# Layer A's keys and queries 2 to 5 as seven-part block products

## The chip, the cores and the metric

The kernel runs on one core of a Trainium2 chip. The core has five engines with a queue each: TensorE (PE; its weight loads are shown apart as PEld), VectorE (DVE), ScalarE (ACT), GpSimd (POOL) and SyncE (SP), which here only issues DMAs. Each queue is worked off in order, and an instruction at the head of a queue that waits holds up all that are behind it. The metric is the device time of one execution in microseconds (us).

## The reference

A decoder trunk of two layers over 1024 tokens of width 1024 in float32. The part that matters here is the first layer's projection of the normed stream `h`, which gives 16 query heads of 64, and keys and values for three branches of attention (compressed blocks, selected blocks, a window) with four groups each:

```python
proj = h @ w_in
splits = [D_MODEL + i * KV_DIM for i in range(7)]
q, kc, vc, ks, vs, kwn, vwn, gl = jnp.split(proj, splits, axis=-1)
...
k_cmp = compress(kvh(kc), pe_k, w1_k, w2_k)
v_cmp = compress(kvh(vc), pe_v, w1_v, w2_v)
```

`compress` cuts the tokens into overlapping blocks of 32, adds `pe`, and sends each through a matrix `w1` of 2048 x 256, a Gelu and a small `w2`. The attention over the three branches, the output projections, the feed-forward parts and the second layer follow; they are the same in both kernels.

## The kernel before

**Numbers in two parts.** A float32 operand is held as a main part (H, a rounded copy made by ACT) and a rest (L, the difference, made by VectorE); `split` makes them. A product is three matmuls: main by main, rest by main, main by rest (`mm3`). The turned stream lies as hT: eight tiles hH0 to hH7 (128 of the 1024 features by 1024 tokens) and eight rests hL0 to hL7.

**Projections.** `proj_T` (line 270) makes 128 columns of `h @ w_in`, turned: for each half of the tokens (512) 8 x 3 matmuls of 128x512 into a bank "mm" (there are six). One chunk of 128 columns holds two heads. Its weights come through `Weights.load` (line 191): one DMA into `wraw`, then wh by ACT and wl by VectorE, in rings of 3, 5 and 5 tiles. The result is split again and stored to DRAM by `store_heads` (line 405) as two tiles, sth and stl, of two buffers each: kS for keys, qS for queries.

**The stage.** hT is made in two halves; the compressed keys' input (kc2) and the values vS of the window follow; then the compression of the keys (`compress`, line 527, with i = 0), the values of the selected blocks, the compressed values' input, and the compression of the values (i = 1). A compression has 16 steps: ACT makes bh (128x256), VectorE bl, both in two buffers, and PE runs six matmuls of 128x256 into two banks, "cmp0" and "cmp1". The second compression is cut into parts by a generator (`steps`), and after each part comes a projection: query chunk 0, key chunk 0 of the selected blocks, key chunk 0 of the window, query chunk 1. Then the pools of the compression close, and key chunks 1 and query chunks 2 to 5 follow with nothing between. Query chunks 6 and 7 come later, between the first steps of the attention.

**Work beside it.** `out_blocks` (line 457) prepares the two output matrices for products that come much later: eight times two tiles ob of 128x1024 are loaded, combined by four subtractions on VectorE, and stored to wS. There are two buffers for each of the two tiles. `next(made)` moves this on by one block, and the loop's order in the text says where. The attention's first loads (queries Q, keys KW and K, bias T) go to tiles of the pools aA0, aA1 and aP, which lie where the tiles of this stage were, so a load waits for the last reader of what lay there.

**What sets the order.** The program is written in the order above; a scheduler then puts each engine's instructions in an order of its own when the kernel is built, and on the chip that order is fixed. `after(x)` asks it to put an instruction no earlier than x.

The seven-part block product is used in later stages already: `cols_steps` (line 1147) makes, from four blocks of a weight matrix (512 features by 128 columns) and prepared sums of the turned rows, four blocks of a result with seven products of 12 matmuls, m1 to m7, in place of eight.

Of the kernel before, what the change touches and what calls it, by code (L numbers as in the profile page):

```python
# [14 lines left out]
OP = mybir.AluOpType  # L15
# [114 lines left out]
def trunk(ctx, tc, I, out):  # L130
# [43 lines left out]
    on_pool, on_vector = [None], [None]  # L174

    def split(H_, L_, src, scale=None, eng=None):

        if scale is None:
            prev = nc.scalar.activation(H_, src, AF.Copy)
            rest = (eng or nc.vector).tensor_sub(L_, src, f32(H_))  # L180
            (on_vector if eng is None else on_pool)[0] = rest
        else:
            prev = nc.scalar.activation(H_, src, AF.Copy, scale=scale)
            nc.vector.scalar_tensor_tensor(L_, src, scale, f32(H_), op0=OP.mult, op1=OP.subtract)
# [85 lines left out]
    def proj_T(w, hT, evac, parts=((0, 512), (512, S))):  # L270

        (wh, wl), (hH, hL) = w, hT
        for lo, hi in parts:
            ps = bank("mm")[:, :hi - lo]
            tk = slice(lo, hi)
            for k in range(KC):
                mm3(ps, (wh[:, k], wl[:, k]), (hH[k][:, tk], hL[k][:, tk]), k == 0, k == KC - 1)
# [150 lines left out]
    with ExitStack() as c:  # L428
# [3 lines left out]
        sv = pool(vctx, "pvt", "right")  # L432
        cctx = ExitStack()
# [23 lines left out]
        def out_blocks(places):  # L457
# [3 lines left out]
            for n in range(9):  # L461
                if ready is not None:
                    dst, ((b11, b12), (b21, b22)), b = ready
# [5 lines left out]
                    for r in range(2):  # L469
                        nc.gpsimd.dma_start(dst[r], b[r])  # L470
                if n == 4:
                    yield
                if n < 8:
                    w, i = (I["a_w_out"][0], I["b_w_out"][0])[n // 4], n % 4
                    b = [places[0].tile([128, 1024], F32, name=f"ob{r}", bufs=2) for r in range(2)]
                    for r in range(2):
                        with after(wts.last):
                            nc.sync.dma_start(b[r], w[(i + 4 * r) * 128:(i + 4 * r + 1) * 128, :])
                    ready = wS[n // 4][i], [(t[:, :512], t[:, 512:]) for t in b], b
                yield  # L480

        def evac_v(i):
            def f(t, ps):
                vt = sv.tile([128, G, DH], F32, name="vt", bufs=2)
# [89 lines left out]

        tok_proj(wv, 304, hT, natural, evac_v(1), range(4, NT))
        places_ = [pool(cctx, "po")]
        made = out_blocks(places_)
# [6 lines left out]
        nc.scalar.activation(gates, gates, AF.Sigmoid)  # L584
        tok_proj(wide(wts, W[:, 1792:2048], 256, 4), 256, hT, natural, evac_v(0))
        next(made)
        for _ in steps:
            pass
        kc2 = blocks_tile()
# [3 lines left out]
        next(made)  # L593

        def evac_k(i, ch):
            def f(ps, tk):
                t = [st.tile([128, 512], F32R, name=n, bufs=2) for n in ("sth", "stl")]
                split(*t, ps)
                store_heads(lambda b, z: kS[i, 2 * ch + b, z], t, tk)
            return f  # L600

        def store_blockind():
            for a in range(2):
                cols = slice(a * 512, (a + 1) * 512)
                raw = sv.tile([16, 512], F32, name="bif", bufs=1)
                nc.gpsimd.dma_start(raw, I["blockind"][:, cols])
                t = st.tile([128, 512], F32R, name="sth", bufs=2)
                nc.scalar.copy(t[:16], raw)
                nc.gpsimd.dma_start(bS[:, cols], f32(t[:16]))

        def evac_q(ch):
            def f(ps, tk):
                t = [st.tile([128, 512], F32R, name=n, bufs=2) for n in ("sth", "stl")]
                split(*t, ps, -DH ** -0.5)
                store_heads(lambda b, z: qS[2 * ch + b, z * 64:(z + 1) * 64], t, tk)
            return f

        def proj_k(i, ch):
            c0 = (1536, 2048)[i] + 128 * ch
# [1345 lines left out]
```

## Time and profile before

| what | value |
|---|---|
| time, median of 3 runs | 2793.09 us (2792.3 to 2796.37) |
| the profiled execution | 2793.83 us, its span 2792.1 us |
| mean granted TensorE clock | 0.997 |
| PE busy | 2738.9 us, 98% of the span |
| VectorE, ACT, POOL busy | 79%, 51%, 50% |
| chain that ended last | PE 85%, VectorE 6%, ACT 2%, issue 2%, DMA 2% |
| DMA | 315.13 MB, mean 113 GB/s |

Busy shares are means over stages. [...] A line such as `bh<-kc,pet 128x256 ... x22 | 16.1, 749 | 10.6 <-PE` is a group of 22 instructions that write bh from kc and pet: 16.1 us in all, 749 ns each, with 10.6 us of idle time of that engine ahead of them that PE ended. In a timeline, a row has start, duration, engine, line, operation, tiles, shapes and count, and in square brackets the engine's idle time before it. "To landing" is the time from the issue of a DMA until its data are there.

### The profile page before, as it was taken

The numbers are of one execution on the slowest core, as the hardware profiler recorded it, in microseconds if no ns is written. First come the engines' busy times: TensorE is split into PE (matmuls) and PEld (weight loads), VectorE is DVE, ScalarE is ACT, GpSimd is POOL, SyncE is SP. The second block draws the span as 40 slices with busy tenths as digits, with TensorE's granted clock in tenths as the row PEclk, the third lists the DMA queues.
The fourth block names the chain that finished last, engine by engine and source line by source line (L and its number), as shares of the span: only waits on it lengthen the run. The fifth ranks groups of instructions, "written<-read, shape, count | busy, mean of one in ns | idle before, by whom it ended". The sixth has DMA issues, their size and how long they took to land.

```text
span 2792.1 us, 43025 instructions
## 1 busy us (share of the span) xinstructions
PE 2738.9 (98%) x14494; PEld 2218.9 (79%) x14494; DVE 2214.7 (79%) x4527; ACT 1426.8 (51%) x3171; POOL 1402.8 (50%) x1454
## 2 busy tenths in 40 slices
PE   9999999999999999999999999999999999999997
PEld 8988676776788888888778888777778888888886
DVE  5453888887889899989875677688898888888987
ACT  5531777775644343333454444577756433343434
POOL 3135655552465566565457787110014756655652
PEclk9999999999999999999999999999999999999999
DMA  8669443224122322232224555786341211112112
GB/s 237 218 196 298 133 128 105 68 62 159 35 76 69 83 65 68 62 77 62 84 80 116 167 156 159 242 257 187 114 174 44 74 58 57 49 57 61 54 42 83
DMA packets 292924, 315.13 MB, mean 113 GB/s; under 512 B 50428, under 2 KB 229677, under 8 KB 292704
## 3 DMA queue, kind: packets, MB, share of 16 engines
q1 hardware_dynamic: 272240, 249.40, 30.5%
q0 software_dynamic: 20464, 62.99, 7.4%
q8 instruction: 115, 1.88, 0.3%
q14 instruction: 105, 0.86, 0.1%
HBM read 243.96 MB, written 81.95 MB: 117 GB/s over the span
## 4 chain that ended last, share of the span: by engine, by line
PE 85%; DVE 6%; ACT 2%; issue 2%; DMA 2%; POOL 1%; SPq 1%; POOLq 0%; DVEq 0%; ACTq 0%
PE ux L1161 18%; PE uy L1161 15%; PE dx L993 8%; PE o L390 7%; PE pt L353 6%; PE dr L993 6%; PE dr L1161 4%; PE mm L230 3%; PE mm L229 3%; PE mm L231 3%; PE s L758 1%; DVE pl L954 1%; PE s L846 1%; PE s L1808 1%; PE s L845 1%
## 5 line engine op out<-in xcount | busy, mean ns | idle before, releaser
L954 DVE TENSOR_TENSOR pl<-oT,ph 128x512 fp32r<-128x512 f32 x340 | 340.2, 1018 | 72.3 <-PE dr L993 17.4
L953 ACT ACTIVATE ph<-oT 128x512 fp32r<-128x512 f32 x346 | 211.8, 628 | 215.6 <-PE ux L1161 53.3
L954 DVE TENSOR_TENSOR pl<-oTb,ph 128x512 fp32r<-128x512 f32 x232 | 214.7, 948 | 27.2 <-PE dr L993 17.4
L953 ACT ACTIVATE ph<-oTb 128x512 fp32r<-128x512 f32 x238 | 145.5, 628 | 168.7 <-PE ux L1161 53.4
L353 PE MATMUL pt<-ident,P 128*128 128x128 f32 x1536 | 228.0, 278 | 3.3 <-DVE pT L356 1.9
L742 POOL TENSOR_SCALAR P<-P,sm,gates 128x384 f32<-128x384 f32 (+7 forms) x256 | 183.2, 727 | 79.3 <-DVE sm L740 54.8
L353 PEld LDWEIGHTS pt<-ident,P 128*128 128x128 f32 x1536 | 172.9, 140 | 61.8 <-issue 43.0
L998 DVE TENSOR_TENSOR xrfx<-xrfx,dr 128x512 f32<-128x512 f32 x320 | 204.2, 679 | 17.8 <-PE dr L993 17.7
L1354 POOL TENSOR_TENSOR oT<-oT,gffn 128x512 f32<-128x512 f32 x92 | 118.9, 1303 | 196.0 <-DMA oT<-in_ffn_w_up_dram 127.7
L998 DVE TENSOR_TENSOR xrfx<-xrfx,dx 128x512 f32<-128x512 f32 x320 | 204.5, 678 | 2.2 <-PE dx L993 2.2
L738 ACT ACTIVATE P<-P,m 128x384 f32<-128x384 f32 (+7 forms) x256 | 171.1, 670 | 36.0 <-DVE m L851 14.9
L356 DVE COPY pT<-pt 128x512 f32<-128x512 f32 (+1 forms) x224 | 143.2, 648 | 44.5 <-PE pt L353 39.8
L1354 POOL TENSOR_TENSOR oTb<-oTb,gffn 128x512 f32<-128x512 f32 x92 | 111.8, 1226 | 130.8 <-DMA oTb<-in_ffn_w_up_dram 79.0
L356 ACT COPY pT<-pt 128x512 f32<-128x512 f32 x192 | 110.1, 578 | 103.8 <-PE pt L353 100.8
L390 PE MATMUL o<-pT,V 128*64 128x256 f32 x1200 | 160.7, 391 | 2.3 <-ACT pT L356 1.5
L1770 ACT ACTIVATE P<-P,st 128x384 f32<-128x384 f32 (+2 forms) x256 | 139.6, 548 | 32.3 <-DVE st L1765 30.4
L1765 DVE CUSTOM_DVE_ANT_0 P<-s,T 128x384 f32<-128x384 f32 (+2 forms) x256 | 112.9, 478 | 10.5 <-PE pt L353 3.0
L390 PEld LDWEIGHTS o<-pT,V 128*64 128x64 f32 x1200 | 73.6, 136 | 51.8 <-issue 9.9
L993 PE MATMUL dx<-ph 128*128 128x512 f32 x320 | 107.5, 390 | 0.8 <-ACT ph L953 0.8
L993 PE MATMUL dx<-ph,pl 128*128 128x512 f32 x320 | 107.0, 389 | 0.0
L847 DVE CUSTOM_DVE_ANT_0 P<-s,T 128x128 f32<-128x128 f32 (+3 forms) x192 | 99.5, 550 | 8.1 <-PE s L846 7.8
L230 PE MATMUL mm<-hL,wh 128*128 128x512 f32 (+1 forms) x272 | 102.6, 378 | 0.0
(623 smaller groups left out, 8040.3 us busy)
## 6 DMA issues: line engine op xcount, KB each, us to landing
qB<-xrfx POOLq DMA_DIRECT2D x96, 256.0 KB, 4.5
oT<-in_ffn_w_up_dram SPq DMA_DIRECT2D x92, 256.0 KB, 2.9
oTb<-in_ffn_w_up_dram SPq DMA_DIRECT2D x92, 256.0 KB, 2.9
Q<-qB SPq DMA_DIRECT2D x40, 512.0 KB, 6.9
wd<-in_ffn_w_down_dram SPq DMA_DIRECT2D x60, 256.0 KB, 2.6
oT<-in_b_w_q_dram SPq DMA_DIRECT2D x48, 256.0 KB, 5.6
K<-kBs SPq DMA_DIRECT2D x40, 256.0 KB, 7.5
wraw<-in_a_w_in_dram SPq DMA_DIRECT2D x18, 512.0 KB, 6.9
```

Of the source, the lines that this page charges most:

```text
L230: nc.tensor.matmul(ps, lh, rl, start=False, stop=False, skip_group_check=bool(shared))
L353: prev = nc.tensor.transpose(ps[:, i * 128:(i + 1) * 128], h, ident)
L356: copy(t[:, :w], ps[:, :w])
L390: mm = nc.tensor.matmul(po[64 * e:64 * e + 64, :256], v[e], t, start=first and lo == i == 0, stop=last and hi == nb and i == len(ops) - 1, ...
L738: nc.scalar.activation(P[:, e, :n], P[:, e, :n], AF.Exp, bias=mm[:, e:e + 1], scale=-1.0, accum_out=sm[:, e:e + 1])
L742: nc.gpsimd.tensor_scalar(P[:, e, :n], P[:, e, :n], sm[:, e:e + 1], gate(e), op0=OP.mult, op1=OP.mult)
L953: nc.scalar.activation(h, src, AF.Copy)
L954: self.last = (eng or nc.vector).tensor_sub(l, src, f32(h))
L993: nc.tensor.matmul(banks[t], part(a, t)[u], b[v], start=z == 0 and onX != 2, stop=z == 2, skip_group_check=True)
L998: nc.vector.tensor_add(xs, xs, banks[t])
L1161: mm = nc.tensor.matmul(b, x[:, i * 128:(i + 1) * 128], ys[i], start=first and (z, i) == (0, 0), stop=(z, i) == (2, 3), skip_group_check=True)
L1354: nc.gpsimd.tensor_mul(v, v, gains[:, k:k + 4].unsqueeze(2).to_broadcast([128, 4, 128]))
```

## The change

Four jobs take the place of eight of the projections, each two chunks wide (256 columns): the selected blocks' keys (0 and 1), the window's keys (0 and 1), queries 2 and 3, queries 4 and 5. A job is one `cols_steps`: its blocks of weights W11, W12, W21, W22 (two chunks by two halves of the features) and their sums are multiplied with halves of hT. B11, B12, B21 and B22 are the halves of the features by halves of the tokens, and need no work; T1 = B12 - B11, T2 = B22 - T1, T3 = B22 - B12 and T4 = B21 - T2 are made once, in two parts each, by `block_sums`. Query chunks 0 and 1 stay as they were, 0 ahead of the second compression and 1 in two halves among the jobs.

```diff
-    def proj_T(w, hT, evac, parts=((0, 512), (512, S))):
+    def proj_T(w, hT, evac, parts=((0, 512), (512, S)), prev=None, where="mm"):
...
     def store_heads(dst, t, cols):
         for b in range(2):
-            for z in range(2):
-                nc.gpsimd.dma_start(dst(b, z)[:, cols], f32(t[z][b * 64:(b + 1) * 64]))
+            nc.gpsimd.dma_start(dst(b)[:, :, cols], f32(t[b * 64:(b + 1) * 64]))
+
+    def two_parts():
+        t = st.tile([128, 2, 512], F32R, name="st", bufs=2)
+        return t, (t[:, 0, :], t[:, 1, :])
...
+        def full():
+            return [f32(t) for t in two_parts()[1]]
+
+        def difference(x, y):
+            t, u = full()
+            with after(on_rest[0]):
+                nc.vector.tensor_sub(t, f32(x[0][:]), f32(y[0][:]))
+            with after(on_rest[0]):
+                nc.vector.tensor_sub(u, f32(x[1][:]), f32(y[1][:]))
+            nc.vector.tensor_add(t, t, u)
+            return t
...
+                if names == "T1":
+                    t = difference(o("B12"), o("B11"))
+                    split(*o("T1"), t)
+                    u, _ = full()
+                    nc.vector.tensor_sub(u, f32(o("B22")[0]), t)
+                    nc.vector.tensor_add(u, u, f32(o("B22")[1]))
+                    split(*o("T2"), u)
+                else:
+                    split(*o(names), difference(*map(o, dict(T3=("B22", "B12"), T4=("B21", "T2"))[names])))
...
+        place = [lambda r: full()]
+        made = out_blocks(place)
...
+        block_sums("T1")
+        block_sums("T3", range(3))
...
         steps = compress(1, kc2, wts)
-        for n, (f, a) in enumerate(((proj_q, (0,)), (proj_k, (0, 0)), (proj_k, (1, 0)), (proj_q, (1,)))):
-            f(*a)
-            if n % 2 == 1:
-                next(made)
-            next(steps, None)
+        proj_q(0)
         for _ in steps:
             pass
+        q1 = wts.load(W[:, 128:256], KC, 128)
...
+        R_, H_, L_ = [[r.tile() for _ in range(n)] for r, n in zip(wts.rings, (3, 4, 4))]
+        cutin = lambda *ts: [t[:, k:k + 512] for t in ts for k in (0, 512)]
+        pairs = Given(list(zip(cutin(*H_[:2]), cutin(*L_[:2]))))
+        wu = Turns(cutin(*R_) + [f32(t) for t in cutin(H_[3])])
...
+        load_job(0)
+        load_job(1)
+        block_sums("T3", (3,))
+        block_sums("T4")
+        fs = [job(n) for n in range(len(jobs))]
...
+                ob = [f32(r.tile()[:]) for r in wts.rings[1:]]
+                place[0] = lambda r: ob[r]
...
+        seq = fs[0][:4] + fs[1][:4] + [lambda: plain(0)] + fs[0][4:6] + [with_load(fs[0][6], 2, False), lambda: plain(1)]
+        seq += fs[1][4:5]
+        end = fs[1][5:]
+        for n in range(2, len(jobs)):
+            seq += [with_load(fs[n][0], len(jobs)), fs[n][1]] + end[:-1] + [with_load(end[-1], n + 1)] + fs[n][2:4] + [with_load(fs[n][4], len(jobs))]
+            end = fs[n][5:]
+        staged(seq + end)
...
-            proj_k(0, 1)
-            proj_k(1, 1)
-            next(made)
-            proj_q(2)
-            next(made)
-            proj_q(3)
-            proj_q(4)
-            next(made)
-            proj_q(5)
-            next(made)
...
-        rKs = Ring("K", [128, S], F32R, [(kA0, 2)])
+        rKs = Ring("K", [128, S], F32R, [(kA1, 2)])
```

`cols_steps`, `Pairs` and `staged` move up in the file; `cols_steps` takes the engine of its sums as an argument, and here it is VectorE. A step m is split in two: `prep` makes the pair of its weights (`wh` by ACT, `wl` by VectorE, in four pairs of half tiles that take turns), `run` its 12 matmuls; `staged` writes the preparation of a step ahead of the matmuls of the one before. The tiles of the weights' rings serve as the jobs' weights, pairs, sums and results. The two tiles st (128 x 2 x 512) hold, in turns, main part and rest of a result on its way to DRAM, the sums' intermediate values, and for the first output matrix a whole block of `out_blocks` (two tiles a block, so one block at a time); for the second output matrix the block lies in one tile of each of the rings wh and wl. A store of a head takes main part and rest in one DMA.

On PE, the second compression: bh and bl are a step's operands, cmp0 and cmp1 its banks, hH and hL the turned rows. Before, around one of its steps:

```order
L229 MATMUL cmp0_1555<-bh_1711,wh1_1686 128x256
L229 MATMUL cmp1_1556<-bh_1711,wh1_1686 128x256
L230 MATMUL mm_1737<-hL6_113,wh2_1732 128x512
L231 MATMUL mm_1737<-hH6_105,wl2_1733 128x512
L229 MATMUL mm_1737<-hH7_106,wh2_1732 128x512
L230 MATMUL mm_1737<-hL7_114,wh2_1732 128x512
L231 MATMUL mm_1737<-hH7_106,wl2_1733 128x512
```

and of the change, two of the steps after the sixth:

```order
L229 MATMUL cmp0_1664<-bh_1774,wh1_1759 128x256
L229 MATMUL cmp1_1665<-bh_1774,wh1_1759 128x256
L230 MATMUL cmp0_1664<-bl_1775,wh1_1759 128x256
L231 MATMUL cmp0_1664<-bh_1774,wl1_1760 128x256
L230 MATMUL cmp1_1665<-bl_1775,wh1_1759 128x256
L231 MATMUL cmp1_1665<-bh_1774,wl1_1760 128x256
L229 MATMUL cmp0_1664<-bh_1784,wh1_1759 128x256
L229 MATMUL cmp1_1665<-bh_1784,wh1_1759 128x256
L230 MATMUL cmp0_1664<-bl_1785,wh1_1759 128x256
```

Projections stood between the steps; now the last ten steps follow one another with nothing between them.

On VectorE, in the same place, the blocks of the first output matrix among the rests bl. Before (L465 to L468 are a block's four subtractions, on tiles ob; wl0_1933 is a projection's weights, stl_1668 the rest of a result on its way to DRAM):

```order
L465 TENSOR_TENSOR ob0_1681<-ob0_1681 128x512
L545 SCALAR_TENSOR_TENSOR bl_1702<-kc2_1326,pet_1550,bh_1701 128x256
L466 TENSOR_TENSOR ob0_1681<-ob1_1682,ob0_1681 128x512
L467 TENSOR_TENSOR ob1_1682<-ob1_1682,ob0_1681 128x512
L468 TENSOR_TENSOR ob1_1682<-ob1_1682 128x512
L180 TENSOR_TENSOR wl0_1933<-wraw2_1931,wh0_1932 128x1024
L180 TENSOR_TENSOR stl_1668<-mm_1642,sth_1667 128x512
L465 TENSOR_TENSOR ob0_1464<-ob0_1464 128x512
L545 SCALAR_TENSOR_TENSOR bl_1712<-kc2_1326,pet_1550,bh_1711 128x256
```

and of the change (L612 to L615 are the four subtractions, on tiles st; wl4_1898 is the rest of job 0's first weights):

```order
L612 TENSOR_TENSOR st_1425<-st_1425 128x512
L180 TENSOR_TENSOR wl3_1875<-wraw0_1873,wh3_1874 128x1024
L694 SCALAR_TENSOR_TENSOR bl_1693<-kc2_1431,pet_1659,bh_1692 128x256
L694 SCALAR_TENSOR_TENSOR bl_1703<-kc2_1431,pet_1659,bh_1702 128x256
L613 TENSOR_TENSOR st_1425<-st_1426,st_1425 128x512
L614 TENSOR_TENSOR st_1426<-st_1426,st_1425 128x512
L694 SCALAR_TENSOR_TENSOR bl_1719<-kc2_1431,pet_1659,bh_1718 128x256
L615 TENSOR_TENSOR st_1426<-st_1426 128x512
L433 TENSOR_TENSOR wl4_1898<-wraw1_1891,wh4_1894 128x512 x2
L694 SCALAR_TENSOR_TENSOR bl_1729<-kc2_1431,pet_1659,bh_1728 128x256
L694 SCALAR_TENSOR_TENSOR bl_1739<-kc2_1431,pet_1659,bh_1738 128x256
L612 TENSOR_TENSOR st_1506<-st_1506 128x512
```

The third block (st_1425, st_1426) and the fourth (st_1506) now stand among the rests of steps 2 to 6, each in the same two tiles as the block before it; before, two blocks one after the other lay in tiles ob of their own (ob0_1681, ob0_1464), among rests with projections between them.

On VectorE again, at the end of the projections, ahead of query chunk 6. Before, where wl2_2595 is the rest of its weights and the tiles ob from ob0_2182 on are blocks of the second output matrix:

```order
L180 TENSOR_TENSOR stl_2136<-mm_2110,sth_2135 128x512
L573 COPY vc_92<-cmp0_1980 64x4x64
L180 TENSOR_TENSOR wl2_2595<-wraw0_2593,wh2_2594 128x1024
L465 TENSOR_TENSOR ob0_2182<-ob0_2182 128x512
L180 TENSOR_TENSOR stl_2169<-mm_2143,sth_2168 128x512
L465 TENSOR_TENSOR ob0_2028<-ob0_2028 128x512
L466 TENSOR_TENSOR ob0_2182<-ob1_2183,ob0_2182 128x512
```

and of the change, where wl4_2682 is the rest of query chunk 6's weights and wh3_2223 with wl3_2224 holds a block of the second output matrix:

```order
L614 TENSOR_TENSOR wl3_2224<-wl3_2224,wh3_2223 128x512
L184 SCALAR_TENSOR_TENSOR st_2483<-wh1_1896,st_2483 128x512
L615 TENSOR_TENSOR wl3_2224<-wl3_2224 128x512
L433 TENSOR_TENSOR wl0_1899<-wraw0_1893,wh0_1895 128x512
L184 SCALAR_TENSOR_TENSOR st_2488<-c_1908,st_2488 128x512
L612 TENSOR_TENSOR wh3_2223<-wh3_2223 128x512
L180 TENSOR_TENSOR wl4_2682<-wraw1_2680,wh4_2681 128x1024
```

The last block's first operation (L612) now stands directly ahead of the weights of query chunk 6; before, their rest was made ahead of all four blocks of the second output matrix.

More of the change, by code (lines that the diff above doesn't have):

```diff
@@ L455, in blocks_weights, with halves, parts, out_blocks @@
             return wts.load(W[:, c0:c0 + 128], KC, 128, eng=eng)
-        def out_blocks(places):
+        lower, upper = slice(0, 512), slice(512, 1024)
+        def halves(t):
+            return [(t[k], c) if isinstance(t, list) else (t[:, c], c) for k, c in enumerate((lower, upper))]
+        def parts(t):
+            return halves(t) if isinstance(t, list) else [(t, slice(0, 1024))]
+        def out_blocks(place):
             ready = None
@@ L573, in compress, with evac_k, f, store_blockind @@
                     nc.vector.tensor_copy(vc[own, :, own], ps2[own].rearrange("p (g d) -> p g d", d=64))
+        def evac_k(i, ch):
+            def f(ps, tk):
+                t, hl = two_parts()
+                split(*hl, ps)
+                store_heads(lambda b: kS[i, 2 * ch + b].rearrange("z d s -> d z s"), t, tk)
+            return f
+        def store_blockind():
+            for a in range(2):
+                cols = slice(a * 512, (a + 1) * 512)
+                t, raw = [t[:16] for t in two_parts()[1]]
+                nc.gpsimd.dma_start(f32(raw), I["blockind"][:, cols])
+                nc.scalar.copy(t, f32(raw))
+                nc.gpsimd.dma_start(bS[:, cols], f32(t))
@@ new lines, in block_sums @@
+        def block_sums(names, rows=range(4)):
+            for i in rows:
+                o = lambda n: ops[n][i]
+                if names == "T1":
[7 more added lines that the diff above has]
+                    split(*o(names), difference(*map(o, dict(T3=("B22", "B12"), T4=("B21", "T2"))[names])))
@@ L588, in trunk @@
             pass
+        next(made)
         kc2 = blocks_tile()
@@ L592, in trunk @@
             bias_skewed(sA, 0, LA, WA + 1, 2 * ch, wts.last)
-        next(made)
[L595 to L619, printed above, removed]
-            proj_T(wts.load(W[:, c0:c0 + 128], KC, 128), hT, evac_k(i, ch))
-        def proj_q(ch):
-            proj_T(wts.load(W[:, 128 * ch:128 * ch + 128], KC, 128), hT, evac_q(ch))
+            next(made)
         with after(prev), after(on_pool[0]):
@@ new lines, in with_load, with prep, plain, run @@
+        def with_load(f, n, blocks=True):
+            def prep():
+                run = f()
+                if n < len(jobs):
+                    load_job(n)
+                if blocks:
+                    next(made, None)
+                return run
+            return prep
+        load_job(0)
[3 more added lines that the diff above has]
+        fs = [job(n) for n in range(len(jobs))]
+        def plain(half):
+            def run():
+                proj_T(q1, hT, evac_q(1), ((512 * half, 512 * half + 512),), where="cmp1")
+                if half == 0:
+                    return
+                ob = [f32(r.tile()[:]) for r in wts.rings[1:]]
+                place[0] = lambda r: ob[r]
+            return run
```

284 lines of the change are left out of this document (167 added, 117 removed).

## The prediction

> **What bounds the kernel now.** First I read the busy time of each engine by stage, for the stage that the change rewrites (layer A's projections, compressions and the first scores):
>
> ```profile
> core 0: us, PE busy (x) PEld busy (x) DVE busy (x) ACT busy (x) POOL busy (x), PEclk, DMA share, GB/s
> 52.00:76.00 24.00, 24.00 (x145) 22.11 (x144) 8.93 (x16) 8.39 (x16) 5.32 (x10) 1.00 1.00 258
> 76.00:98.00 22.00, 20.83 (x171) 20.42 (x171) 11.46 (x16) 14.05 (x21) 2.57 (x5) 1.00 0.84 247
> 98.00:107.00 9.00, 9.00 (x77) 9.00 (x76) 0.22 (x1) 1.78 (x4) 2.14 (x5) 1.00 0.67 239
> ...
> 107.00:139.00 32.00, 32.00 (x166) 27.34 (x165) 19.84 (x26) 17.50 (x27) 1.96 (x5) 1.00 0.55 174
> 139.00:211.00 72.00, 72.00 (x382) 60.73 (x381) 35.99 (x50) 26.27 (x38) 26.18 (x50) 1.00 0.65 194
> 211.00:270.00 59.00, 59.00 (x264) 48.90 (x263) 19.34 (x29) 8.39 (x13) 28.61 (x57) 1.00 0.94 308
> ```
>
> PE is busy all the time but 1.2 us between 76 and 98, at the full granted clock; VectorE (DVE) is half idle; DMA is nearly full only after 211. Next, what PE waits for between 46 and 300 us, the longest two:
>
> ```profile
> PE mm L229 <- ACT wh L179: 0.8, 1, 0.8
> ...
> PE mm L230 <- DVE wl L180: 0.4, 1, 0.4
> ```
>
> So the stage costs what PE's matmuls cost, and every matmul taken out counts, provided that PE never waits. The duration of a matmul (0.39 us) is no price, because they overlap; the price is the distance of two starts, which PE's timeline gives:
>
> ```profile
> 58.70 0.39 PE L230 MATMUL mm<-hL,wh 128*128 128x512 f32 x1
> 58.93 0.39 PE L231 MATMUL mm<-hH,wl 128*128 128x512 f32 x1
> 59.15 0.39 PE L229 MATMUL mm<-hH,wh 128*128 128x512 f32 x1
> 59.38 0.39 PE L230 MATMUL mm<-hL,wh 128*128 128x512 f32 x1
> ...
> 84.45 0.28 PE L231 MATMUL cmp<-bh,wl 128*128 128x256 f32 x1
> 84.57 0.28 PE L229 MATMUL cmp<-bh,wh 128*128 128x256 f32 x1
> ```
>
> (59.38 - 58.70) / 3 = **0.227 us** for 512 columns, 0.12 us for 256.
>
> **What goes.** Each of the four jobs covers two 128-column chunks: 7 products of 12 matmuls, where 2 chunks took 96. 4 x 12 = 48 matmuls of 512 columns fewer: 48 x 0.227 = **-10.9 us**. POOL issues 40 DMAs fewer, but nothing on PE waited for POOL: nothing. I look for what PE will newly wait for, in the order of the program.
>
> **A. Sums of the turned rows, up to 107 us.** VectorE gets T1, T2 and three quarters of T3 here: 4 x 7 + 3 x 4 = 40 operations of 128x512.
>
> ```profile
> 108.47 0.68 DVE L465 TENSOR_TENSOR ob<-ob 128x512 f32<-128x512 f32 x1
> 109.08 1.22 DVE L180 TENSOR_TENSOR wl<-wraw,wh 128x1024 fp32r<-128x1024 f32 x1
> ...
> 111.94 0.69 DVE L467 TENSOR_TENSOR ob<-ob,ob 128x512 f32<-128x512 f32 x1
> 112.66 0.69 DVE L468 TENSOR_TENSOR ob<-ob 128x512 f32<-128x512 f32 x1
> ```
>
> One costs 0.61 us, or 0.72 us behind the one that it needs; I use 0.64. That is 26 us on top of the 8.9 + 11.5 + 0.2 = 20.6 us of the first three windows, 47 of 55 us. They stand between the rests (wl, bl) that PE waits for. Free if they fall into gaps; if VectorE is late by one or two groups of 2 to 3 us, up to 5 us. I take **+2** (0 to 5), near the free end, since the total still fits.
>
> **B. The second compression.** Before, its 16 steps (bh, bl, six matmuls of 256) lay among the 192 matmuls of four projections. Now q0 (10.9 us) runs ahead of them, 24 matmuls of job 0 lie among steps 4 and 5, and steps 6 to 15 follow bare. The rows that price a step:
>
> ```profile
> L180 DVE TENSOR_TENSOR wl<-wraw,wh 128x1024 fp32r<-128x1024 f32 x17 | 20.8, 1225 | 37.1 <-ACT wh L179 37.1
> L544 ACT ACTIVATE bh<-kc,pet 128x256 fp32r<-128x256 f32 x22 | 16.1, 749 | 10.6 <-PE cmp L231 10.3 <-DVE kc L445 0.4
> L545 DVE SCALAR_TENSOR_TENSOR bl<-kc,pet,bh 128x256 fp32r<-128x256 f32 x22 | 14.1, 663 | 4.6 <-ACT bh L544 4.6
> ```
>
> PE needs 6 x 0.12 = 0.72 us for a step. But bh and bl have two buffers, and ACT waited for PE's release of one (10.3 us in that row, unseen because PE had other work). Bare, a buffer goes round in 0.64 (three starts and an end, 3 x 0.12 + 0.28, after bl) + 0.75 + 0.66 + some 0.05 = 2.1 us: 1.05 us a step. Steps 2 and 3 lose 1.5 us that way, steps 10 to 15 6 x 0.33 = 2 us.
>
> Between the bl rests VectorE's queue also holds the a_w_out blocks, and these are now one deep: a block sits in the only two staging tiles (st), so the next one is loaded after the stores of the last have landed. Before there were two sets (ob).
>
> ```profile
> L470 POOL DMA_DIRECT2D wS<-ob x16: 540/574/574, 111.2 to 250.6; - x16
> ...
> DMA to landing us min/median/max: 2.9/5.1/9.9
> ...
> L478 SPq DMA_DIRECT2D ob<-in_b_w_out_dram x8: 340/514/1531, 210.1 to 236.1; - x8
> ...
> DMA to landing us min/median/max: 3.4/7.3/16.3
> ```
>
> A store (2.9 to 5.1 us) and a load (3.4 to 7.3) take 6.3 to 12.4 us; I take 8. Counting from the end of the values' block projection: the second block's first rows are done at 2.1, the third block can start at 10 and has its first rows done at 14.6, so the fourth starts at 22.5, with its second half at 24.5; bl of step 7 stands behind it and comes at 26, where PE wanted it at 22.5. Steps 7 to 9 lose 4 us. The fourth block's stores then have to land before the two small blockind loads, whose casts stand in ACT's queue ahead of the last two bh: another 2 us. Last, PE's vc matmuls wait for the two Gelus:
>
> ```profile
> L552 ACT ACTIVATE hid<-cmp 128x256 f32<-128x256 f32 x4 | 1.5, 380 | 0.7 <-PE cmp L231 0.7
> ```
>
> 2 x 0.38 and a latency, 0.9 us. Together **+10.4**: by the shortest landings 5, by the median ones 14.
>
> [...]
>
> **C. T4 and the last row of T3.** After the compression VectorE has 45 rows to go (splits of jobs 0 and 1, their sums, 20 for T3 and T4): 45 x 0.64 = 29 us, while PE has 16 short matmuls and 108 of 512 columns, 26 us, until T4 is read to its end. Also ACT's copy for T4's last row stands behind the copy of T3's result. PE waits about 2 us there and 1 us more for the split of job 0's last product, whose buffer is released one product earlier: **+3** (0.5 to 6).
>
> **D. Job 3 to q6.** The b_w_out blocks go through a single pair of weight tiles, loaded from when q1 is done (X). Of PE's work then 204 matmuls are left before q6: 204 x 0.227 = 46.3, plus 0.5 of early scores: X + 47. VectorE makes q6's wl right behind the first operation of the fourth block, which needs four loads and three stores one after another. With 5.5 for a load, 5.7 for store and issue and 2 to 3 us of VectorE between, that is X + 49, and wl X + 50; by the medians X + 57; by the shortest well before. I take **+3** (0 to 10). These bytes are crowded: 4.2 MB of blocks in, 3.7 out, 12 head stores of 0.52, 3.3 MB of weights and first loads, 17.5 MB in 47 us = 372 GB/s, where the trace's fullest window had:
>
> ```profile
> 211.00:230.00 19.00, 19.00 (x85) 15.73 (x84) 9.24 (x13) 3.69 (x5) 8.43 (x16) 1.00 1.01 338
> ```
>
> **E. Start of the attention.** The T loads now wait for T4's tiles, and K comes behind them. Before, loads were issued 7 us ahead of TW and 16 us ahead of their use (253.95, 260.86, 269.83 in the timelines):
>
> ```profile
> 253.95 3.85 SPq L685 DMA_DIRECT2D T<-sA  x4
> ...
> 260.86 0.51 POOL L689 TENSOR_SCALAR_AFFINE_SELECT TW<-T 128x384 f32<-128x384 f32 x1 [3.13 <-DMA T<-sA]
> ...
> 269.83 0.29 DVE L759 CUSTOM_DVE_ANT_0 P<-cmp,TW 128x128 f32<-128x128 f32 x1 [4.46 <-PE cmp L758]
> ```
>
> q6 covers 10.9 us of it: **0** (-1 to +3). The rest of the program is unchanged but for its tiles' places.
>
> **Sum.** -10.9 + 2 + 10.4 + 3 + 3 + 0 = **+7.5 us** against the profiled execution's 2793.83 (span 2792.1 and 1.7 around it): 2801.3. That execution stands 0.7 above the median of the runs: **2800.6**, say 2801.
>
> **The rivals.**
> 1. *The covers hold: faster.* The place is the same, VectorE's queue at step 7 and before q6. If a store and a load take 6.3 us and VectorE's fillers find gaps, B is 5, C 1, A and D 0: -10.9 + 6 = -5 us or better, 2783 to 2788. For it: all engines but PE have room in the sums. Against it: B's buffer loop and Gelus (4.4 us) depend on no DMA. It decides at 11 us of new waits in all.
> [...]
> 3. *Much slower: DMA takes over.* Landings as the medians: B 14, D 10, A and C 6: +19, 2807 to 2816. For it: 372 GB/s asked where 338 was the most. If PE then stands for some us, its clock could fall too. The trace has no such fall in idle times like the 1.2 us above (1.00 throughout). [...]
> 4. *It doesn't do what it says* (some matmuls as many as before): the order of the instructions has 48 fewer, so no chance is kept.
>
> **How the numbers follow.** Forecast (2796 to 2806) 0.43, rival 1 0.20, rival 2 0.23, rival 3 0.14. About 0.2%, 5.6 us around the median, is what a measurement can tell from no change: faster is rival 1, 0.20; rival 2 and the forecast's lower edge lie within, 0.30; slower 0.50. The range 2786 to 2813 leaves out half of rival 1's lower part and rival 3's upper part.
>
> **What would show it.** Right: PE idle in the second compression about 9 us, released by DVE bl and ACT bh, VectorE there waiting for DMA st<-in_a_w_out; PE idle 1 to 3 us at T4; VectorE waiting for wh<-in_b_w_out ahead of q6's wl. Wrong: PE busy through the compression (B falls), PE at q6 waiting 10 us (rival 3), or idle in the attention that was not there.

## The result, and the profile after

The changed kernel takes 2819.07 us (median of 5 runs, 2816.19 to 2820.52), the kernel before beside it 2792.3 us: a ratio of 1.0093, 95% interval 1.0078 to 1.0107. It is slower by 26 us, where 8.5 were forecast and 2813 was the upper end of the range. The profiled execution has a span of 2817.2 us, 25.1 more than before's.

First the busy time by stage, over about the stages that the prediction showed:

```profile
core 0: us, PE busy (x) PEld busy (x) DVE busy (x) ACT busy (x) POOL busy (x), PEclk, DMA share, GB/s
...
76.00:98.00 22.00, 22.00 (x184) 21.85 (x183) 19.16 (x30) 13.62 (x22) 2.70 (x5) 1.00 0.86 237
...
107.00:144.00 37.00, 37.00 (x183) 31.30 (x183) 19.65 (x27) 16.36 (x25) 2.88 (x7) 1.00 0.53 169
144.00:172.00 28.00, 23.77 (x124) 19.63 (x122) 18.47 (x29) 15.70 (x25) 6.50 (x13) 0.88 0.49 168
172.00:212.00 40.00, 38.10 (x184) 30.16 (x184) 31.22 (x52) 14.96 (x27) 6.90 (x12) 1.00 0.52 145
212.00:272.00 60.00, 48.95 (x204) 39.12 (x204) 33.31 (x53) 19.13 (x33) 17.23 (x32) 0.94 0.81 260
272.00:300.00 28.00, 28.00 (x124) 23.36 (x123) 11.98 (x52) 11.43 (x40) 15.53 (x30) 0.94 0.96 304
300.00:350.00 50.00, 40.48 (x260) 29.91 (x259) 38.45 (x191) 34.90 (x126) 31.89 (x67) 0.93 0.61 170
```

Up to 144 us PE has no gap, though VectorE is at 87% between 76 and 98. Then there are three holes: the second compression (4.2 us idle in 144:172), the end of the jobs (11 us in 212:272; another 1.9 us lie in 172:212) and the start of the attention (9.5 us in 300:350). In these three rows and in 272:300 the granted clock is below 1.00, which it was in no row of this stage before. What PE waits for between 46 and 330 us, the longest first:

```profile
PE mm L465 <- ACT wh L514: 8.6, 2, 5.9
PE pt L354 <- POOL P L979: 6.1, 1, 6.1
PE cmp L230 <- DVE bl L694: 3.6, 6, 1.9
PE mm L465 <- DVE vp L524: 1.8, 1, 1.8
...
PE mm L465 <- ACT wh L432: 1.0, 1, 1.0
```

From PE's timelines come three marks: the first step of the second compression (before 145.7, after 144.2), the end of query chunk 7 (281.9 and 299.2), the end of the span. So 1.5 us are gained ahead of the compression, 18.8 are lost from there to the end of the projections (155.0 us for 136.2, though 10.9 us of matmuls are gone: 29.7 us of new loss), and 7.8 from there to the end. The sum is 25.1. Of the 7.8 us, 5.4 lie ahead of the first matmul of the output products (`dx<-ph`, 395.7 us after the end of chunk 7, before 390.3); the work behind it is the same in both kernels.

**The end of the jobs.** VectorE's timeline of the changed kernel; L612 and L613 are the first operations of a block of the second output matrix, in square brackets how long VectorE stood:

```profile
254.88 0.69 DVE L612 TENSOR_TENSOR wh<-wh 128x512 f32<-128x512 f32 x1 [5.95 <-DMA wh<-in_b_w_out_dram]
257.50 0.69 DVE L613 TENSOR_TENSOR wh<-wl,wh 128x512 f32<-128x512 f32 x1 [1.92 <-DMA wl<-in_b_w_out_dram]
258.10 0.68 DVE L540 TENSOR_TENSOR wh<-wh,mm 128x512 f32<-128x512 f32 x1
...
268.65 0.69 DVE L612 TENSOR_TENSOR wh<-wh 128x512 f32<-128x512 f32 x1 [6.26 <-DMA wh<-in_b_w_out_dram]
269.26 1.22 DVE L180 TENSOR_TENSOR wl<-wraw,wh 128x1024 fp32r<-128x1024 f32 x1
270.40 0.68 DVE L524 TENSOR_TENSOR vp<-vp,mm 128x512 f32<-128x512 f32 x1
```

ACT's, in the same place:

```profile
258.87 0.63 ACT L183 ACTIVATE st<-wh 128x512 fp32r<-128x512 f32 x1 [9.87 <-DVE wh L540]
...
259.93 0.58 ACT L514 ACTIVATE wh<-mm 128x512 f32<-128x512 f32 x1
```

and PE's:

```profile
253.56 1.07 PE L465 MATMUL mm<-T1h,wl 128*128 128x512 f32 x4
260.56 1.65 PE L465 MATMUL mm<-T3h,wh 128*128 128x512 f32 x3 [5.93 <-ACT wh L514]
```

Read upwards, this is one chain. PE waits for ACT's copy L514 of a result out of its bank; that stands behind the split L183, the split waits for VectorE's sum L540 (the last one of job 2), and that stands behind the third block, whose load had been issued only at 249.0, when the block before it had been stored. At 268.65 it happens again, ahead of query chunk 6's weights. VectorE's waits between 200 and 275 us add it up:

```profile
DVE wh L612 <- DMA wh<-in_b_w_out_dram: 17.0, 3, 6.3
...
DVE wh L613 <- DMA wl<-in_b_w_out_dram: 3.4, 2, 1.9
```

**The clock.** PE's timeline in the second compression, ahead of the stop at 146 and behind it:

```profile
145.31 0.28 PE L229 MATMUL cmp<-bh,wh 128*128 128x256 f32 x1
145.43 0.28 PE L230 MATMUL cmp<-bl,wh 128*128 128x256 f32 x1
...
148.38 0.38 PE L230 MATMUL cmp<-bl,wh 128*128 128x256 f32 x1 [1.93 <-DVE bl L694]
...
149.60 0.41 PE L231 MATMUL cmp<-bh,wl 128*128 128x256 f32 x1
149.81 0.41 PE L230 MATMUL cmp<-bl,wh 128*128 128x256 f32 x1
```

Starts 0.12 us apart become 0.21 apart. The slowing begins at 148.93 and ends at 152.34. Windows cut so show all stretches between 46 and 330 us with a clock below 1.00:

```profile
145.52:148.93 3.41, 1.36 (x9) 0.95 (x8) 2.96 (x4) 1.10 (x2) 0.54 (x1) 1.00 0.62 217
148.93:152.34 3.41, 3.33 (x13) 2.80 (x12) 2.84 (x5) 2.54 (x4) 1.08 (x2) 0.50 0.78 235
...
162.58:165.99 3.41, 3.41 (x17) 3.01 (x15) 1.85 (x3) 1.75 (x3) 1.33 (x3) 0.50 0.41 163
165.99:169.40 3.41, 3.03 (x19) 2.39 (x18) 1.98 (x3) 2.98 (x6) 0.71 (x2) 1.00 0.08 19
...
230.85:234.26 3.41, 1.80 (x10) 1.36 (x8) 0.87 (x2) 0.63 (x2) 0.00 (x0) 1.00 0.93 334
234.26:237.68 3.42, 2.39 (x10) 1.99 (x11) 2.58 (x4) 1.53 (x4) 1.18 (x2) 1.00 0.79 252
237.68:241.09 3.41, 3.41 (x16) 2.81 (x15) 2.07 (x4) 2.04 (x5) 1.18 (x2) 1.00 0.61 149
...
258.16:264.98 6.82, 4.42 (x10) 3.47 (x11) 4.24 (x8) 2.76 (x5) 4.27 (x9) 0.50 0.61 146
...
271.81:275.22 3.41, 3.41 (x10) 2.66 (x9) 1.70 (x2) 0.81 (x1) 2.50 (x5) 0.50 0.89 282
...
312.77:319.60 6.83, 3.87 (x13) 3.50 (x14) 0.00 (x0) 1.58 (x5) 4.04 (x10) 0.50 1.05 286
```

In these windows the granted clock is 1.00 or 0.50: three times it was 0.50 for 3.41 us, once for 6.82 and once for 6.83. Ahead of each of these five stretches PE was idle in part or wholly: of the 3.41 us before their starts, in order of time, it was busy for 1.36, 2.17, 0.00, 1.62 and 0.23. By an estimate from the rows, the slowing costs at most half of PE's busy time in the five halved stretches, (3.33 + 3.41 + 4.42 + 3.41 + 3.87) / 2 = 9.2 us, up to a quarter of the 36 us (25.1 + 10.9) that the change loses.

**The start of the attention.** SP's timeline of the changed kernel (QM is a copy of the first group's queries, T its bias):

```profile
308.97 0.63 SPq L913 DMA_DIRECT2D QM<-qS  x1
309.65 2.02 SPq L922 DMA_DIRECT2D T<-sA  x4
```

and what waits for it on POOL:

```profile
315.02 0.23 POOL L931 COPY C<-T 128x31 f32<-128x31 f32 x1 [6.41 <-DMA T<-sA]
```

QM reads qS and waits on SP until all stores of the queries have landed; the last ones, of query chunk 7, were issued between 301.0 and 303.5. T has nothing to do with them, but stands behind QM. Before, QM went out 9.2 us after the end of chunk 7 (291.09), now 9.8 after: the chain is about as long as it was. A likely reason for the stop, not shown by itself, is that the attention had more other work behind chunk 7 then, since the scheduler now puts its first scores earlier, between the last projections: by ACT's timelines the first exponential comes 20.6 us ahead of the end of chunk 7, before 10.5.

### The profile page after: what moved, and what is told of

The parts are those of the page before. It is cut to its first block, busy times and chain, and to the rows that moved or that the text cites. A ratio compares the mean times of both kernels' runs of the same rounds, so it can differ in the third digit from the quotient of the medians.

```text
span 2817.2 us, 43094 instructions
## 1 busy us (share of the span) xinstructions
PE 2741.3 (97%) x14446; PEld 2217.9 (79%) x14446; DVE 2277.8 (81%) x4635; ACT 1450.0 (51%) x3219; POOL 1380.7 (49%) x1414
## 4 chain that ended last, share of the span: by engine, by line
PE 79%; DVE 8%; DMA 4%; issue 4%; ACT 2%; POOL 2%; SPq 0%; POOLq 0%; DVEq 0%; ACTq 0%
PE ux L465 18%; PE uy L465 15%; PE dx L1200 8%; PE o L391 7%; PE pt L354 6%; PE dr L1200 5%; PE dr L465 4%; DVE pl L433 2%; PE s L995 1%; PE mm L229 1%; PE mm L230 1%; PE s L1083 1%; PE mm L231 1%; PE dx L465 1%; PE s L1918 1%
## 5 line engine op out<-in xcount | busy, mean ns | idle before, releaser
L432 ACT ACTIVATE ph<-oT 128x512 fp32r<-128x512 f32 x346 | 212.1, 627 | 217.2 <-PE ux L465 54.2
L432 ACT ACTIVATE ph<-oTb 128x512 fp32r<-128x512 f32 x238 | 145.1, 627 | 171.9 <-PE ux L465 54.3
L1880 ACT ACTIVATE P<-P,st 128x384 f32<-128x384 f32 (+2 forms) x256 | 139.3, 546 | 30.1 <-DVE st L1875 28.1
L432 ACT ACTIVATE ph<-wd 128x512 fp32r<-128x512 f32 x80 | 50.2, 628 | 90.3 <-PE ux L465 48.5
```

What stands on the lines that cost most here:

```text
L432: nc.scalar.activation(h, src, AF.Copy)
L1880: nc.scalar.activation(P[:, e, :n], P[:, e, :n], AF.Exp, bias=stats[:, slot, hh:hh + 1], scale=-1.0, accum_out=stats[:, slot, 4 + hh:5 + hh])
```

## The experiments

Three causes are proposed. **Theory 1**: blocks of the output matrices that are one deep hold up VectorE's queue, in the compression and at the end of the jobs. **Theory 2**: T waits only because QM does. **Theory 3**, at first the rival of 1 for the compression: its bare steps go round two buffers too slowly, whatever else VectorE does. The times:

| run | median us | ratio to before, 95% interval | second compression us | first compression to end of chunk 7 us | rest us | of it up to the output products us |
|---|---|---|---|---|---|---|
| before | 2792 to 2795 | 1 | (projections among it) | 206.0 | 2510.2 | 390.3 |
| changed | 2819.07 | 1.0093 [1.0078, 1.0107] | 27.6 | 223.3 | 2518.0 | 395.7 |
| e1_no_b_blocks | 2808.31 | 1.0047 [1.0033, 1.0061] | 26.0 | 213.4 | 2516.9 | 392.1 |
| e2_no_a_blocks | 2814.16 | 1.0068 [1.0049, 1.0086] | 27.5 | 220.5 | 2513.1 | 396.8 |
| e4_t_first | 2813.83 | 1.0071 [1.0055, 1.0088] | 26.8 | 220.1 | 2514.8 | 392.6 |
| e5_all_three | 2804.48 | 1.0037 [1.0023, 1.0050] | 27.0 | 214.6 | 2511.4 | 391.1 |
| e6_three_late | 2796.52 | 1.0003 [0.9994, 1.0013] | 28.2 | 206.4 | 2512.6 | 392.6 |
| y2_blocks_in_attention | 2833.18 | 1.0140 [1.0123, 1.0157] | 28.1 | 206.3 | 2546.6 | 426.0 |
| y4_cover_back | 2847.46 | 1.0184 [1.0166, 1.0201] | - | 212.2 | 2550.3 | 430.5 |
| e7_spread | 2812.78 | 1.0070 [1.0057, 1.0083] | - | 217.3 | 2515.3 | 396.3 |
| e8_buffers | 2811.43 | 1.0063 [1.0050, 1.0077] | 19.7 | 212.5 | 2515.1 | 395.0 |
| y5_cover_tfirst_b_later | 2810.79 | 1.0058 [1.0045, 1.0072] | - | 209.9 | 2520.7 | 397.0 |
| e9_three_causes_out | 2792.79 | 0.9991 [0.9982, 1.0000] | 19.4 | 202.1 | 2512.1 | 392.0 |
| y6_complete | 2797.84 | 1.0011 [1.0002, 1.0020] | 20.0 | 201.6 | 2518.6 | 395.1 |

The last four columns are from PE's timelines of one execution each. The second compression is counted from its first matmul to the first of its values' product; a dash stands where more than the 24 matmuls of job 0 lie in it. The rest runs from the end of query chunk 7 to the end of the span; the last column ends at the first matmul of the output products (`dx<-ph`). What follows that matmul is the same work in every run and took 2116.3 to 2124.9 us, so a few us in the rest alone show nothing. The stretch ahead of the first compression is in no column; it ended between 74.7 and 80.7 us. Medians of the kernel before, run beside each group, moved between 2792.3 and 2795.2, so a difference between groups of runs is uncertain by up to 3 us.

**Blocks and T, one at a time.** The first four runs:

```diff
-                if blocks:
-                    next(made, None)
...
-        for _ in made:
-            pass
```

> The blocks of the second output matrix (b_w_out) are left out of the projections: no loads into the single pair of weight tiles, no subtractions on VectorE, no stores; the matrix goes to wS uncombined in the attention, by DRAM-to-DRAM copies. Theory 1 (a one-deep block stands in VectorE's queue ahead of what PE needs): the changed kernel's PE idles of 5.93, 0.69 and 1.79 us between 253 and 272 us go, and with them some 5 us of matmuls at half speed behind them (granted clock 0.83 and 0.91 in 250:270 and 270:290): 11 to 14 us, 2805 to 2808 us. Rival (the two staging tiles st and their stores hold ACT up, the 2.64 us stop at 232 is one of those, and would do so anyway): less than 4 us, 2815 or more.

Measured: 10.8 us less than the changed kernel's 2819.07, just under theory 1's range. From the compression's last step to the end of chunk 7 it takes 112.7 us in place of 127.4, so **14.7 us hang on these blocks**: all waits for L514 are gone, the one at 232 (2.64 us) too, so that one was no separate matter of the staging tiles. The run takes the blocks' loads, subtractions and stores away together; that their depth of one is what costs is read from VectorE's waits above, and no run tried a deeper place for them. It is less in the total because the copies of the matrix, which were to go in the attention, were put at the very start of SP's queue by the scheduler, and weights came late (PE waited 2.5 us in 76:98 for ACT's wh, at a granted clock of 0.84).

```diff
-            for n in range(9):
+            for n in range(4, 9):
...
-                if n == 4:
-                    yield
...
-        next(made)
```

> The blocks of the first output matrix (a_w_out) are left out of the compressions; the matrix goes to wS uncombined in the attention. Theory 1 (VectorE waits for a block's load ahead of a rest bl in the bare second compression): the PE idles of 1.93 and 0.92 us go, and most of the half-speed matmuls after them (granted clock 0.97 and 0.86 in 130:150 and 150:170, 3.4 us): 4 to 7 us, 2812 to 2815 us. Rival (the loop over two buffers of bh and bl alone makes the bare steps slow): 0 to 3 us, and PE still waits 0.2 us in each of the last steps.

Measured: 4.9 us less, inside what theory 1 expected, but not where it expected it: the compression takes 27.5 us in place of 27.6. The jobs gain 7.0 us (120.4 in place of 127.4), where PE stood 4.0 us for L514 in place of 8.6; why the second matrix's blocks came less late there is not shown. With both matrices' blocks out (e5, e6) the jobs take 109.4 us. The rest, too, is 4.9 us shorter, but behind the start of the output products, where nothing was edited. Against that, copies stood at the start of SP's queue here as well, and up to the second compression 7.4 us were lost. For the compression theory 1 falls.

```diff
+                if g > 0:
+                    load_q(g, 1)
-                load_q(g, 1)
                 load_v(1, g, 1)
                 load_bias(g, 0)
+                if g == 0:
+                    load_q(g, 1)
```

> The first group's bias loads T stand ahead of the load QM in SP's queue; nothing is left out. In the changed kernel QM waits on SP until the last stores of query chunk 7 have landed (issued to 303.5, QM at 308.97), T follows at 309.65 and lands at 315.0, and PE stands 6.15 us with a granted clock of 0.91 over 310:350. Theory 2 (the T loads wait in the queue only because QM does): the stop goes, 6 to 9 us, 2810 to 2813 us. Rival (QM's own landing, 6 us later than before, stops the masked scores a little further on, or the attention has only as much other work as before): 0 to 3 us.

Measured: 5.2 us less, a little under theory 2's range. The profiled execution is 6.3 us shorter: 3.1 of them lie between chunk 7 and the output products, the others in the projections, which this edit doesn't touch; why they are shorter is not shown. PE's wait for the weights P falls from 6.1 to 3.5 us. But it is 1.9 us in e1 and 2.0 in e8, which leave T behind QM. So theory 2 is borne out in part, and its size is not firm.

> All three edits together: no blocks of either output matrix among the projections (both matrices uncombined), T ahead of QM. If the three waits are apart and make up the loss: 11 + 4 + 6 to 14 + 7 + 9 us less, 2789 to 2798 us, so about the time of the kernel before or a little less. If removing one wait only uncovers the next (staging tiles, loop over two buffers, sums of the turned rows on VectorE): above 2802 us.

Measured: 2804.48, in the rival's range, but for a reason of its own: the copies at the start (16 of them now). PE waited 7.2 us in 76:98, and in the jobs the stops were gone but for 0.7 us.

**The same without that flaw, and with nothing left out.** In e6 the copies are held behind the loads of the attention's keys. In y2 all blocks are made in the attention; in y4 chunks 0 and 1 are cover for the compression besides: their matmuls stand among its steps.

```diff
+                    with after(kw_last[0]):
+                        nc.sync.dma_start(wS[n // 4][n % 4, r], w[...])
```

> As the run of all three edits (no blocks of either output matrix among the projections, both matrices uncombined; T ahead of QM), but the DRAM-to-DRAM copies of the two matrices are held until the attention, where they stood in that run at the very start of SP's queue and delayed the loads of the weights (PE waited 7.2 us between 76 and 98 with a granted clock of 0.77 there). If that stop came from the copies alone, it goes: 7.2 us and some 4 us of half speed less, 2791 to 2796 us. Rival (the stop comes from the order without the blocks): 2802 or more.

> Nothing left out: the blocks of both output matrices are made in the attention, in 16 half blocks through two tiles of 128x512, and T stands ahead of QM. The projections are as in the run before. 64 subtractions of 128x256 more on VectorE in the attention, some 24 us by the 0.37 us that such an operation would take at half the length. If VectorE has room there (83% busy between 400 and 600): 2791 to 2798 us. Rival (each block waits for its load at the head of VectorE's queue, or VectorE becomes the bound): 2800 to 2815 us.

> As the run before it, and query chunks 0 and 1 are put back among the steps of the second compression, in halves of 24 matmuls; nothing left out. Theory (the bare steps cost PE their idles, 3.6 to 4.4 us, and the half-speed matmuls after them, 2 to 4 us): 5 to 8 us less than the run before it. Rival: the chunk 1 was cover for VectorE's sums T4 among the jobs, and what is gained before 185 us is lost there: within 2 us of the run before it.

e6 measured 2796.52, level with before: blocks and T together are worth 22.6 us. It leaves the compression as it was, at 28.2 us, with a DMA share there of 0.12 in place of 0.49. So what the bare steps lose is not a matter of DMA:

```profile
144.70:172.90 28.20, 23.43 (x121) 19.25 (x120) 19.39 (x31) 14.71 (x23) 1.18 (x2) 0.88 0.12 39
```

The stop at step 2 is there as in the changed kernel (1.99 us for 1.93): in place of a block, the rest of a projection's weights, a split and two operations of the sums stand ahead of its bl on VectorE.

y2's 2833.18 is a failure that says the same as the changed kernel: the half blocks in the attention are one deep too, and VectorE's waits of y2 between 290 and 620 us show it standing for them at the head of its queue (L638 and L639 are a half block's first operations):

```profile
DVE ob L638 <- DMA ob<-in_a_w_out_dram: 12.2, 5, 4.3
...
DVE ob L638 <- DMA ob<-in_b_w_out_dram: 4.5, 4, 2.5
...
DVE ob L639 <- DMA ob<-in_a_w_out_dram: 2.1, 3, 1.0
DVE ob L639 <- DMA ob<-in_b_w_out_dram: 1.8, 1, 1.8
```

20.6 us of VectorE's waiting, and the rest grew by 34 us against e6, 33.4 of them ahead of the output products; the 64 subtractions themselves are in that as well, and the two are not told apart. y4 contains y2's loss; up to the end of chunk 7 it took 5.9 us more than y2. (Its profiled execution, 2839.05, is the fastest of four that reach to 2850.56.) Its rival came true: with chunk 1 gone as cover, PE waited 5.0 us for T4's main part and 4.3 us for L514.

**What the compression waits for.**

```diff
+                    with after(prevs.get(n, [None])[0]):
+                        mm3(ps[:], (wh[:, k], wl[:, k]), (hH[k][:, tk], hL[k][:, tk]), k == 0, k == KC - 1)
```

> The changed kernel with query chunk 0's matmuls spread over the second compression: 15 of its 48 ahead of it, the others in threes behind steps 1 to 3 and 6 to 13; nothing left out. Theory (the bare steps, not the a_w_out blocks, cost PE the 11 us that the compression takes over its matmuls, since leaving those blocks out left it at 27.5 us): from the first step to the values' last matmuls PE is nearly without stops and at a granted clock of 1.00, 5 to 9 us less than the changed kernel, 2810 to 2814 us. Rival (VectorE is late there whatever stands between, because of the blocks' waits in its queue): 0 to 3 us less.

```diff
-                    bh = cp.tile([128, G, 64], F32R, name="bh", bufs=2)
-                    bl = cp.tile([128, G, 64], F32R, name="bl", bufs=2)
+                    bh = cp.tile([128, G, 64], F32R, name="bh", bufs=4)
+                    bl = cp.tile([128, G, 64], F32R, name="bl", bufs=4)
```

> bh and bl have four buffers in place of two; to make room, T3's third row is not made and its second is used twice (a part of the result is wrong by that, and VectorE has 5 operations less). Theory (in the bare steps a buffer of bh or bl goes round in twice the 1.13 us that a step takes there): the steps go at the 0.75 us of ACT's bh, so the ten bare steps take 3 to 4 us less, with less at half speed: 3 to 6 us, 2813 to 2816 us. Rival (ACT and VectorE are busy with weights and pairs, so more buffers give nothing): within 2 us of the changed kernel.

e7 gained 6.3 us, as theory 3 expected, and e8 7.6. e8, with the first matrix's blocks still in it, takes 19.7 us for the compression in place of 27.6, at a clock of 1.00; here are the changed kernel's compression and then that of e8:

```profile
144.20:171.80 27.60, 23.39 (x121) 19.27 (x119) 18.27 (x29) 15.49 (x24) 6.31 (x12) 0.88 0.49 168
```

```profile
148.70:168.40 19.70, 17.43 (x121) 15.99 (x119) 14.58 (x23) 14.22 (x23) 5.45 (x10) 1.00 0.48 147
```

So **7.9 us of the compression are the two buffers**. That is more than the 3 to 6 expected, since the half speed goes as well: at most 3.4 us of the 7.9, for the two halved stretches. A stop of 2.08 us for bl at step 2 is left in e8, with no halved stretch behind it, so not all of that is the buffers' merit; e9 and y6, with four buffers, show the same (1.8 and 2.4 us, clock 1.00). Groups of the changed kernel in that stretch say the same from ACT's side: of 14 bh, ACT stood 8.2 us ahead of them until PE freed a buffer.

```profile
L693 ACT ACTIVATE bh<-kc,pet 128x256 fp32r<-128x256 f32 x14 | 10.3, 738 | 8.2 <-PE cmp L231 8.2
```

**All three out.** y5 joins e7's cover, T first and the second matrix in the attention; e9 and y6 have the buffers of e8 in place of the cover, with T3's third row made in room that is free after the compression; e9 leaves the second matrix uncombined.

> The cover of the run with query chunk 0 spread, T ahead of QM, and the second matrix's blocks as eight half blocks in the attention, each one's first subtraction held on VectorE until a turn after its load's; the first matrix's blocks stay in the compressions; nothing left out. If the three costs are apart (15 + 3 + 6 us) and the held blocks cost the attention under 3 us: 2790 to 2797 us, about the kernel before or 2 to 3 us less. If VectorE still waits for loads or POOL for VectorE in the attention, as in the run with 16 half blocks: 2805 or more.

> The three causes taken out together: bh and bl with four buffers (T3's third row is made after the compression, in room of its own, so all values of the projections are right), T ahead of QM, and the second matrix's blocks left out (that matrix is uncombined in wS, by copies in the attention); the first matrix's blocks stay. If the causes are these three and nearly apart (15 + 5 + 8 to 11 us): 2786 to 2790 us, that is 4 to 8 us less than the kernel before. If the five more operations on VectorE after the compression, or the stops at T4, take it back: 2794 to 2799 us.

> As the run before it, with nothing left out: the second matrix's blocks are made in the attention as eight half blocks, their subtractions on POOL (57% busy there), each held back until a turn after its load. If POOL has room: 0 to 3 us more than the run before it, 2787 to 2793 us, faster than both kernels or level with the one before. If POOL's queue then holds up the scaling of the weights P: 4 to 10 us more, 2792 to 2798 us.

y5 missed, by two things: PE waited 4.1 us for T4's main part (3.6 in e7, whose cover it has), and with the held half blocks on VectorE the way to the output products took 4.4 us more than e6's; another 3.7 us lie in the unchanged work behind. e9 measured 2792.79, 26.3 us less than the changed kernel and 2.4 us less than the kernel before beside it (the interval ends at 1.0000); it was expected 4 to 8 less. y6, which leaves nothing out, lands at 2797.84, 0.1% over the kernel before and 5.0 us over e9. Its projections are as short as e9's; in the profiled executions its way from chunk 7 to the output products is 3.1 us longer, and the unchanged work behind 3.4. Its time is inside the range that was expected if POOL held up the weights P, and PE does stand 5.4 us for them, but all of this ends 100 us ahead of POOL's first subtraction for a block:

```profile
294.63 0.33 PE L354 MATMUL pt<-ident,P 128*128 128x128 f32 x1 [4.53 <-POOL P L1001]
```

```profile
395.74 0.73 POOL L639 TENSOR_TENSOR ob<-ob 128x256 f32<-128x256 f32 x1
```

So the subtractions are not its cause; the number came true without that mechanism, and what makes y6 slower than e9 is not shown. No complete version beat the kernel before. What e9's projections still lose, in its waits of PE between 77 and 280 us:

```profile
PE cmp L230 <- DVE bl L694: 1.8, 1, 1.8
PE mm L465 <- ACT c L523: 1.0, 1, 1.0
PE mm L465 <- DVE T4l L180: 1.0, 2, 0.8
PE mm L465 <- ACT vp L523: 0.7, 1, 0.7
```

Its projections take 202.1 us where 206.0 - 10.9 = 195.1 would be all of the gain. PE is idle for 5.1 us of them, and one halved stretch (3.41 us at 0.50) costs, by an estimate from its length, 1.7 more.

## Why the prediction was wrong

The sign was right and the place of every loss but one was named, but the size was a third of what came.

- **What goes (-10.9)**: about right. e9's projections are 3.9 us shorter than before's, with 5.1 us of idle time (before 1.2) and 1.7 us of half speed in them; without these the difference is 9.5.
- **A (+2)**: it came out at -1.5. VectorE took the 26 us of sums in its gaps (it was busy for 48.4 us between 52 and 107, before for 20.6), as the free end of the bounds had it, and the 1.2 us stop that before had there went as well.
- **B (+10.4)**: the size was right by luck and the mechanism wrong. 96 x 0.12 + 24 x 0.227 = 17.0 us of matmuls took 27.6: 10.6. PE stood idle for 4.2 us of it, where about 9 were to be the sign of being right. And of the 10.4 forecast, 6 were VectorE's waits for the first matrix's blocks and the blockind casts, and only 3.5 the loop over two buffers. Without the blocks the compression stayed at 27.5; with four buffers it fell by 7.9. The loop had been priced as if PE kept its speed, and step 2's stop too small, which stands with the blocks, without them and with four buffers (1.9, 2.0 and 2.1 us in the changed kernel, e2 and e8): a bare step took 1.13 us in e6 (12 matmuls from 162.22 to 164.48) where 1.05 had been reckoned, and steps behind a stop ran at half speed.
- **C (+3)**: about right in size, 1.7 us of stops, some 2 with the restarts behind them (the four matmuls from 197.11 on, right behind the 0.69 us stop, took 1.54 us, the four from 190.15 on 1.07). PE stopped 1.0 us for the pair of job 0's last product (ACT wh L432), as forecast. The other 0.7 us was not for VectorE's rows of T4, but for ACT's copy of T3's result out of the bank (c L523), into which T4's product adds.
- **D (+3, bounds 0 to 10)**: this is the step that failed. e1 puts it at 14.7. First, the chain of loads and stores was priced at 5.5 and 5.7 us, under the 7.3 that the quoted row had as the median load. By the medians the weights' rest was to come at X + 57; it came at 269.26, and X, the end of chunk 1, was 213.1: X + 56. The prediction had that number and chose X + 50 instead. In the changed kernel these loads took 6.4 and 7.3 us to landing (medians of the two tiles), the stores 4.5 and 5.5. Second, only the fourth block was followed to what stands behind it (chunk 6's weights, and behind them the sum L524, for which PE stood 1.8 us). The third one's wait was the dear one: behind it stood the last sum of job 2, ACT's split and copy behind that, and PE's next bank behind the copy (5.9 us). Third, both stops were followed by half speed: PE's 4.42 busy us from 258.16 to 264.98 and 3.41 from 271.81 to 275.22. The terms as measured, -10.9 - 1.5 + 10.6 + 2 + 14.7 + 7.8, come to 22.7 of the 25.1; the jobs' 109.4 us without both matrices' blocks, 18.0 less, say that some 3 us more of the jobs hang on the first matrix's.
- **E (0, bounds -1 to +3)**: failed too; it came out at 5.4, and the other 2.4 us of the rest lie in the unchanged work, within its spread. The T loads that the prediction looked at, for the first scores, were not late. The four behind QM were, and what seems to have covered their chain before was attention work that now runs earlier. T first gave 3.1 of the 5.4 back (e4), the second matrix's blocks left out without it 3.6 (e1), both together 3.1 to 4.6 (e6, e9, e5). The last 0.8 to 2.3 us are not explained.
- **The rivals**: nearest was rival 3 (B 14, D 10, together +19, chance 0.14), for the right reason in D, landings as the medians. It was too low: E had no price in it, and the clock (at most 9.2 us) stood there only as a thing that could happen. Rival 1's covers held in A alone. Rival 2, level with before, came no nearer. Short landings were not what the end of the jobs showed: the load issued at 262.10 let VectorE go on at 268.65, 6.5 us later, with a DMA share of 0.96 from its issue until then.
- **The clock**: the prediction judged from 1.2 us of idle time spread over 22 us that it would not fall. Here 0.50 was granted behind single stops of 1.93 and 1.79 us. But behind the 2.64 us stop at 232 it was 1.00, while the same stop in e4, only 1.88 us long, was followed by 0.50; what decides this is not shown:

```profile
230.97:234.38 3.41, 1.53 (x9) 1.19 (x8) 1.77 (x3) 1.60 (x3) 0.78 (x2) 1.00 0.86 311
234.38:237.79 3.41, 3.41 (x9) 2.65 (x9) 2.11 (x4) 1.15 (x2) 1.18 (x3) 0.50 0.62 159
```

## What to carry to other kernels

A product with fewer matmuls pays in operands that have to lie somewhere: here T1 to T4 and the jobs took the room of double buffers, and the jobs no longer covered a loop over two buffers, so that 36 us were lost for 10.9. Before such a change is priced, list every buffer that gets shallower, give its round trip by the medians of the landings, and follow what stands behind each wait on its in-order queue through to the next engines, not only behind the last one. Where PE gets bare stretches, a stop can cost more than its own length: here 3.41 us at 0.50 followed stops of 1.93 and 1.79 us, by an estimate from these rows up to 1.7 us each, but stops of 2.64 us here and 2.08 in e8 cost nothing of the kind.

## What the hardware showed that was not expected

The granted clock was halved behind much shorter stops than thought: it was 0.50 for 3.41 us behind stops of 1.93, 0.92 and 1.79 us, and 1.00 behind one of 2.64 us. Matmuls of 256 columns started 0.21 us apart then, in place of 0.12. What decides whether a stop is followed by half speed, and how much idle time suffices, is not shown: PE was busy 2.17 of 3.41 us from 159.17 to 162.58, where the bare steps had some 0.2 us of idle time each beside the 0.92, and was halved behind it; it was busy 1.80 from 230.85 to 234.26 and was not.
